# Differential scores from four 128-row matmuls, and a block's combination queued behind the next block's maxima

## The chip, the cores and the metric

One core of a Trainium2 chip runs the kernel; the other cores are idle. The metric is the device time of one execution in microseconds (us), median of several runs. The core has five engines with queues of their own: TensorE (PE, with weight loads, PEld, that overlap its matmuls), VectorE (DVE), ScalarE (ACT), GpSimd (POOL) and SyncE (SP), which here issues DMAs. A tile framework makes the semaphores, and its scheduler orders each engine's instructions before the run by its own estimates, following the order of the program text where nothing speaks against it. `keep_in_program_order` pins one instruction behind the instruction that was written just before it for the same engine.

## The reference

A two-layer encoder on 1024 tokens of width 1024, in float32. Layer 0 is a pooling mixer beside latent attention, layer 1 differential attention; each layer ends with a SwiGLU block. Only layer 1's attention is touched:

```python
s = jnp.einsum('bqhmd,bkhmd->mbhqk', qblk, k).astype(jnp.float32) * scale + bias[None, None]
p = jax.nn.softmax(s, axis=-1)
a = (p[0] - lam * p[1]).astype(v.dtype)
return jnp.einsum('bhqk,bkhe->bqhe', a, v)
...
o = rmsnorm(o, subln_g) * (1.0 - lam_init)
```

There are 8 heads; each has two maps (m = 0, 1) of 64 features, a bias that falls with distance, and values of 128 features.

## The kernel before

Matrix products keep float32 accuracy by splitting: each operand becomes hi (its rounding to fp32r) plus lo (the rest), and a product is hi x hi + hi x lo + lo x hi, three fp32r matmuls (`mm3`, lines L162 to L164). ACT makes hi by a copy, DVE lo by a subtraction.

In the attention of layer 1 the outer loops run over 8 heads h and 2 halves hf of the queries, 16 groups in all, four blocks of 128 queries (qt) each. A group begins with the scores of its first block (`diff_scores`), then runs the values of the group before (`diff_values`: per 128 keys four transposes of the blocks' weights e, L506, a hi and a lo copy, L509 and L510, and an `mm3` with V), and in between and after it the scores of its other three blocks. `fill(n)` puts n units of projection work for the next head (`qkv_work`; a unit is one `mm3` of one k-tile, 24 units a group) between these steps. Work handed to `defer` (lo subtractions, mostly) is issued by later fills, one a unit.

Scores of one block: for each half of the keys, two PSUM banks (m = 0, 1) out of three that rotate (`ps_s`). L1263 multiplies QS[m] = [q hi; q lo] (64 rows each) with KS[m] = [k hi; k hi]: 128 rows. L1266 adds q hi x k lo, with KL on rows 64m to 64m+63: 64 rows. L1268 on DVE adds the bias, takes the maximum and frees the bank. After both halves DVE makes the negative maximum (L1276), ACT the exponentials (L1281) with their sums l. Then DVE forms c = -lam l0 / l1 (L1285, L1286), and e0 + c e1 is made: on POOL for the first three blocks of a group (L1290, L1291), on DVE for the fourth (L1288). The transposes of the next group read it.

The operands come from `k_split` (L1151 scales, L1155 hi, an SP DMA that copies the hi half to the other 64 partitions, L1157 lo) and `q_split` (L1161, L1166, L1167, which writes lo straight to the other 64 partitions). `sub_norm` normalises a group's output; L1314 is its reciprocal of l0s, L1339 (`rest`) a deferred lo of its result. L136 is POOL's lo of projection weights, L134 the load of their raw chunks on SP's queue; three raw tiles rotate.

Of the kernel before, what the change touches and what calls it, by code (L numbers as in the profile page):

```python
# [34 lines left out]
def f(ap):  # L35
    return ap.bitcast(F32)
# [7 lines left out]
def encoder_trunk(ctx: ExitStack, tc: tile.TileContext, A: dict):  # L44
# [22 lines left out]
    def half(hf):  # L67
        return slice(hf * HT, (hf + 1) * HT)
# [4 lines left out]
    def tmp(name):  # L73
        return tpool.tile([P, HT], F32, tag="tm", name=name, bufs=6)
# [1061 lines left out]
    def defer(work):  # L1136

        later.append(work)

    def settle():  # L1140
        while later:
            later.pop(0)()

    def k_split(h, hf, ps):
        if hf == 0:
            heads[h]["k"] = (
                [qk.tile([P, T], F32R, tag=f"KS{m}", name=f"KS{m}_{h}", bufs=2) for m in range(2)],
                qk.tile([P, T], F32R, tag="KL", name=f"KL{h}", bufs=2))
        KS, KL = heads[h]["k"]
        t = tmp(f"kt{h}_{hf}")  # L1150
        dve.tensor_tensor(t, ps, rb[:, half(hf)], ALU.mult)  # L1151
        for m in range(2):
            r = slice(64 * m, 64 * m + 64)
            o = slice(64 - 64 * m, 128 - 64 * m)
            act.copy(KS[m][r, half(hf)], t[r, :])  # L1155
            nc.sync.dma_start(f(KS[m][o, half(hf)]), f(KS[m][r, half(hf)]))
            defer(lambda r=r, m=m: dve.tensor_tensor(KL[r, half(hf)], t[r, :], f(KS[m][r, half(hf)]), ALU.subtract))  # L1157

    def q_split(h, hf, ps):
        t = tmp(f"qt{h}_{hf}")  # L1160
        dve.scalar_tensor_tensor(t, ps, float(2.0 ** (h - 2)), rb[:, half(hf)], ALU.mult, ALU.mult)  # L1161
        QS = [qk.tile([P, HT], F32R, tag=f"QS{m}", name=f"QS{m}_{h}_{hf}", bufs=3) for m in range(2)]
        for m in range(2):
            r = slice(64 * m, 64 * m + 64)
            o = slice(64 - 64 * m, 128 - 64 * m)
            act.copy(QS[m][r, :], t[r, :])  # L1166
            defer(lambda r=r, m=m, o=o: dve.tensor_tensor(QS[m][o, :], t[r, :], f(QS[m][r, :]), ALU.subtract))  # L1167
        heads[h].setdefault("q", []).append(QS)

    def v_scale(h, hf, ps):  # L1170
        t = tmp(f"vt{h}_{hf}")
# [72 lines left out]
    def fill(n):  # L1244
        for _ in range(n):
            if later:
                later.pop(0)()
            if next(work, 0) == 0:
                settle()
                return  # L1250

    def diff_scores(h, qt, l0s):
        KS, KL = heads[h]["k"]
        slope = float(2.0 ** -(h + 1))
        c = blk(qt % 4)
        k0 = 896 - P * qt
        e = [at.tile([P, T], F32, tag=f"e{m}", name=f"e{m}_{h}_{qt}", bufs=(6, 2)[m]) for m in range(2)]
        mx = [spool.tile([P, 2], F32, tag="mx", name=f"mx{m}_{h}_{qt}") for m in range(2)]
        QS = heads[h]["q"][qt // 4]
        for hf in range(2):  # L1260
            ps = [ps_s(f"s{m}_{h}_{qt}_{hf}") for m in range(2)]
            for m in range(2):
                pe.matmul(ps[m], QS[m][:, c], KS[m][:, half(hf)], start=True, stop=False)  # L1263
            for m in range(2):
                r = slice(64 * m, 64 * m + 64)
                pe.matmul(ps[m], QS[m][r, c], KL[r, half(hf)], start=False, stop=True)  # L1266
            for m in range(2):
                dve.tensor_tensor_reduce(  # L1268
                    out=e[m][:, half(hf)], in0=ps[m], in1=nd[:, k0 + hf * HT : k0 + hf * HT + HT], scale=1.0,
                    scalar=-3.0e38, op0=ALU.add, op1=ALU.max, accum_out=mx[m][:, hf : hf + 1])  # L1270
            if hf == 0:
                fill(1)
        out = []
        for m in range(2):
            nm = spool.tile([P, 1], F32, tag="nm", name=f"nm{m}_{h}_{qt}")
            dve.tensor_scalar(nm, mx[m][:, 0:1], mx[m][:, 1:2], -slope, ALU.max, ALU.mult)  # L1276
            if m == 0:
                l = l0s[:, qt % 4 : qt % 4 + 1]
            else:
                l = spool.tile([P, 1], F32, tag="l", name=f"l1_{h}_{qt}")  # L1280
            act.activation(e[m], e[m], AF.Exp, bias=nm, scale=slope, accum_out=l)  # L1281
            out.append((e[m], l))
        (e0, l0), (e1, l1) = out
        c1 = spool.tile([P, 1], F32, tag="c1", name=f"c1_{h}_{qt}")
        dve.reciprocal(c1, l1)  # L1285
        dve.scalar_tensor_tensor(c1, l0, nlam, c1, ALU.mult, ALU.mult)  # L1286
        if qt % 4 == 3:
            dve.scalar_tensor_tensor(e0, e1, c1, e0, ALU.mult, ALU.add)  # L1288
        else:
            pool.tensor_scalar(e1, e1, c1, 0.0, ALU.mult, ALU.add)  # L1290
            pool.tensor_tensor(e0, e0, e1, ALU.add)  # L1291
        return e0

    def diff_values(h, hf, es, l0s, between):
# [8 lines left out]
    def sub_norm(h, hf, o, l0s, last=False):  # L1303


        nat = ps_t(f"on{h}_{hf}")
        for j in range(4):
            pe.transpose(nat[:, blk(j)], o[:, blk(j)], ident)
        ss = spool.tile([P, 4], F32, tag="ss", name=f"ss{h}_{hf}", bufs=2)
        sq = tmp(f"osq{h}_{hf}")  # L1310
        for j in range(4):
            act.activation(sq[:, blk(j)], nat[:, blk(j)], AF.Square, accum_out=ss[:, j : j + 1])
        r0 = spool.tile([P, 4], F32, tag="r0", name=f"r0_{h}_{hf}", bufs=2)
        dve.reciprocal(r0, l0s)  # L1314
        v = spool.tile([P, 4], F32, tag="v", name=f"v_{h}_{hf}")
        dve.tensor_tensor(v, ss, r0, ALU.mult)
        dve.tensor_tensor(v, v, r0, ALU.mult)
        dve.tensor_scalar(v, v, 1.0 / P, EPS, ALU.mult, ALU.add)
        r = spool.tile([P, 4], F32, tag="r", name=f"r_{h}_{hf}")
        pool.tensor_tensor(r, v, mhalf, ALU.pow)  # L1320
        dve.tensor_tensor(r, r, r0, ALU.mult)
        y = tmp(f"yn{h}_{hf}")
        dve.tensor_tensor(
            y.rearrange("p (a b) -> p a b", a=4), nat.rearrange("p (a b) -> p a b", a=4),
            r.unsqueeze(2).broadcast_to([P, 4, P]), ALU.mult)
        yield
        yt = ps_t(f"yt{h}_{hf}")
        for j in range(4):
            pe.transpose(yt[:, blk(j)], y[:, blk(j)], ident)
        if h in y_t:  # L1330
            yh, yl = (t[:, half(hf)] for t in y_t[h])
        else:
            yh = at.tile([P, HT], F32R, tag="pth", name=f"yh{h}_{hf}", bufs=3)
            yl = at.tile([P, HT], F32R, tag="ptl", name=f"yl{h}_{hf}", bufs=3)
        act.activation(yh, yt, AF.Identity, scale=gsub)


        def rest():
            dve.scalar_tensor_tensor(yl, yt, gsub, f(yh), ALU.mult, ALU.subtract)  # L1339
            if h not in y_t:  # L1340
                nc.sync.dma_start(f(ysp[h, 1, :, half(hf)]), f(yl))

        if last:
            rest()
        else:
            defer(rest)
        if h not in y_t:
            nc.sync.dma_start(f(ysp[h, 0, :, half(hf)]), f(yh))
# [28 lines left out]
    for h in range(NH):  # L1377
        for hf in range(2):
            l0s = spool.tile([P, 4], F32, tag="l0s", name=f"l0s_{h}_{hf}")
            es = [diff_scores(h, 4 * hf, l0s)]  # L1380

            def between(kt):
                if h < NH - 1 or hf or kt > 3:
                    fill(1)
                if kt == 3:
                    es.append(diff_scores(h, 4 * hf + 1, l0s))

            if prev is None:
                fill(8)
                es.append(diff_scores(h, 1, l0s))  # L1390
                fill(4)
                es.append(diff_scores(h, 2, l0s))
                fill(4)
                es.append(diff_scores(h, 3, l0s))
                fill(8)
            else:
                if h < NH - 1 or hf:
                    fill(3)
                pv = diff_values(*prev, between)
                fill(1)  # L1400
                norm_o = sub_norm(*pv)
                next(norm_o)
                es.append(diff_scores(h, 4 * hf + 2, l0s))
                fill(2)
                es.append(diff_scores(h, 4 * hf + 3, l0s))
                if h == NH - 1 and hf == 1:
                    fill(1000)
                    ya.release()
                    yb = new_pool("yb", "right")
                    load_y(yb, range(4, 8))  # L1410
                fill(6)
                next(norm_o, None)
            prev = h, hf, es, l0s
        if h == NH - 2:
# [6 lines left out]
            for o in ftr:  # L1421
                nc.sync.dma_start(hT[o], hsp[o])
            work = out_work()
    norm_o = sub_norm(*diff_values(*prev, lambda kt: fill(2)), last=True)
    next(norm_o)
    fill(1000)
# [218 lines left out]
```

## Time and profile before

| what | us |
|---|---|
| median of 3 runs | 2613.55 (2607.86 to 2615.01) |
| profiled execution | 2614.45 |
| its span, first to last instruction | 2612.7 |
| layer 1's attention, from its first groups to the end of its last scores | 1215 to 1842 of the span |

The rows below are from that one execution. Times in a timeline are microseconds from the span's start; "busy" of PE runs to modelled ends of overlapping matmuls, so starts tell more than lengths. A bracket behind a row is the idle time of that engine before it and what ended it. "issue" as releaser means that the profile shows nothing that the engine waited for.

### The profile page before, as it was taken

How to read it: one execution, taken by the hardware profiler on the slowest of the kernel's cores; microseconds unless marked ns; L12 is line 12 of the kernel's file. 1: busy time of each engine (PE TensorE's matmuls, PEld its weight loads, DVE VectorE, ACT ScalarE, POOL GpSimd, SP SyncE). 2: the span in 40 equal slices, each digit the busy share in tenths (PEclk: the TensorE clock that was granted, in tenths of full speed). 3: DMA queues.
4: the chain of work that ended last, by engine and by line, in shares of the span. 5: the costliest groups of instructions: out<-in, count | busy, mean ns of one | idle time of the engine just before them, and what ended most of it. 6: DMA issues, size and time to landing. Idle time of an engine off the chain costs nothing. (4 is left out here: it accounts for less than half of the span.)

```text
span 2612.7 us, 31389 instructions
## 1 busy us (share of the span) xinstructions
PE 2517.5 (96%) x11334; PEld 1989.8 (76%) x11334; DVE 1688.7 (65%) x2882; ACT 1060.5 (41%) x1866; POOL 757.8 (29%) x582
## 2 busy tenths in 40 slices
PE   8999999899999999999999999999989999999997
PEld 6787887678888888886666666666778888887886
DVE  7567777776666664554776776776586666666544
ACT  4236667533333331244555445554453333332222
POOL 4224444232222200033434344343343222220002
PEclk9999999999999999999999999999999999999998
DMA  3110001622222152321111111114352222215321
GB/s 130 37 45 15 17 9 43 163 95 73 91 79 85 69 173 81 113 98 60 37 45 37 45 41 33 41 42 165 117 141 97 81 89 77 93 56 183 113 73 65
DMA packets 127148, 205.50 MB, mean 79 GB/s; under 512 B 11280, under 2 KB 54288, under 8 KB 126992
## 3 DMA queue, kind: packets, MB, share of 16 engines
q1 hardware_dynamic: 120656, 187.76, 21.6%
q0 software_dynamic: 6336, 15.73, 2.4%
q8 instruction: 89, 1.46, 0.2%
q14 instruction: 67, 0.55, 0.1%
HBM read 145.25 MB, written 46.66 MB: 73 GB/s over the span
## 5 line engine op out<-in xcount | busy, mean ns | idle before, releaser
L163 PE MATMUL d<-al,whi_d 128*128 128x512 f32 x576 | 224.8, 390 | 0.4 <-DVE al L932 0.3
L164 PE MATMUL d<-ah,wlo_d 128*128 128x512 f32 x576 | 224.2, 389 | 0.0
L162 PE MATMUL d<-ah,whi_d 128*128 128x512 f32 x576 | 224.2, 389 | 0.0
L970 DVE TENSOR_TENSOR hd<-hd,d 128x512 f32<-128x512 f32 x160 | 109.6, 686 | 169.1 <-PE d L164 168.6
L776 POOL TENSOR_TENSOR s<-s,raw_a 128x512 f32<-128x512 f32 x88 | 116.3, 1322 | 327.6 <-DVE wlo_s L796 223.3
L509 ACT CAST pth<-pt 128x512 fp32r<-128x512 f32 x256 | 145.5, 586 | 155.5 <-PE pt L506 152.9
L510 DVE TENSOR_TENSOR ptl<-pt,pth 128x512 fp32r<-128x512 f32 x256 | 169.9, 686 | 53.1 <-ACT pth L509 51.6
L1268 DVE CUSTOM_DVE_ANT_0 e<-s,nd 128x512 f32<-128x512 f32 x256 | 169.2, 686 | 42.3 <-PE s L1266 39.5
L776 POOL TENSOR_TENSOR s<-raw_a,raw_a 128x512 f32<-128x512 f32 x88 | 116.8, 1327 | 250.8 <-DVE wlo_s L796 194.4
L795 ACT CAST whi_s<-s 128x512 fp32r<-128x512 f32 x142 | 88.3, 622 | 235.0 <-PE p L163 218.2
L1281 ACT ACTIVATE e<-e,nm 128x1024 f32<-128x1024 f32 x128 | 146.4, 1147 | 69.5 <-DVE nm L1276 69.4
L506 PE MATMUL pt<-ident,e 128*128 128x128 f32 x1024 | 155.8, 280 | 9.2 <-POOL e L500 4.7
L506 PEld LDWEIGHTS pt<-ident,e 128*128 128x128 f32 x1024 | 124.6, 144 | 48.0 <-DVE ptl L510 11.2
L1290 POOL TENSOR_SCALAR e<-e,c 128x1024 f32<-128x1024 f32 x48 | 57.4, 1196 | 273.4 <-ACT pth L509 97.3
L163 PEld LDWEIGHTS d<-al,whi_d 128*128 128x128 f32 x576 | 108.1, 188 | 24.5 <-DVE al L932 2.2
L162 PEld LDWEIGHTS d<-ah,whi_d 128*128 128x128 f32 x576 | 108.1, 188 | 22.3
L164 PEld LDWEIGHTS d<-ah,wlo_d 128*128 128x128 f32 x576 | 108.1, 188 | 22.3
L954 ACT CAST whi_d<-raw_d 128x512 fp32r<-128x512 f32 x72 | 44.4, 621 | 195.4 <-PE d L163 187.3
L795 ACT CAST whi_a<-raw_a 128x512 fp32r<-128x512 f32 x106 | 65.5, 621 | 134.5 <-PE p L163 131.5
L1263 PE MATMUL s<-KS,QS 128*128 128x512 f32 x256 | 96.0, 423 | 24.1 <-DVE mx L1268 23.2
L1291 POOL TENSOR_TENSOR e<-e,e 128x1024 f32<-128x1024 f32 x48 | 116.9, 2435 | 3.4
L796 DVE TENSOR_TENSOR wlo_s<-s,whi_s 128x512 fp32r<-128x512 f32 x142 | 115.7, 816 | 1.5 <-ACT whi_s L795 1.4
(501 smaller groups left out, 6998.5 us busy)
## 6 DMA issues: line engine op xcount, KB each, us to landing
raw_a<-in_w_gate_dram SPq DMA_DIRECT2D x88, 256.0 KB, 2.8
raw_a<-in_w_up_dram SPq DMA_DIRECT2D x88, 256.0 KB, 2.6
asp<-u SPq DMA_DIRECT2D x40, 512.0 KB, 2.9
raw_d<-in_w_down_dram SPq DMA_DIRECT2D x80, 256.0 KB, 2.7
araw<-asp SPq DMA_DIRECT2D x40, 512.0 KB, 4.0
hd<-hs POOLq DMA_DIRECT2D x16, 512.0 KB, 8.3
acc_f<-sq_f POOLq DMA_DIRECT2D x28, 256.0 KB, 4.1
hT<-in_xT_dram SPq DMA_DIRECT2D x16, 256.0 KB, 5.4
```

The source lines that it names most:

```text
L162: pe.matmul(ps, sh, mh, start=start, stop=False, skip_group_check=onto)
L163: pe.matmul(ps, sh, ml, start=False, stop=False, skip_group_check=onto)
L164: pe.matmul(ps, sl, mh, start=False, stop=stop, skip_group_check=onto)
L506: pe.transpose(pt[:, blk(j)], es[j][:, blk(kt)], ident)
L509: act.copy(hi, pt)
L510: dve.tensor_tensor(lo, pt, f(hi), ALU.subtract)
L776: pool.tensor_tensor(t, r[ff, a], r[ff, b], op)
L795: pin(act.copy(hi, self.raws[ff, n]))
L796: pin(dve.tensor_tensor(lo, self.raws[ff, n], f(hi), ALU.subtract))
L1268: dve.tensor_tensor_reduce(out=e[m][:, half(hf)], in0=ps[m], in1=nd[:, k0 + hf * HT : k0 + hf * HT + HT], scale=1.0, scalar=-3.0e38, op0=A ...
L1281: act.activation(e[m], e[m], AF.Exp, bias=nm, scale=slope, accum_out=l)
L1291: pool.tensor_tensor(e0, e0, e1, ALU.add)
```

## The change

`k_split` builds X[m], 128 partitions: k hi on rows 64m and up, k lo on the other 64, which DVE writes there directly; the DMA that doubled k hi goes. `q_split` builds two operands a map, [hi; hi] and [lo; lo]; the second half of each is a DMA on SP's queue from the first. `diff_scores` multiplies both with X[m]: (hi + lo) x (hi + lo), four products in two 128-row matmuls a map and key half. For the second half's queries of every head but the first, the split (`q_operands`) is called only after the next head's first scores, with its casts and subtractions pinned. The fourth block's combination (`combine`) is put on a list, `tail`, and called by `end_tail` in the next group's first scores, behind the maxima of the first key half, or after the loops; its reciprocal and that of `sub_norm` are pinned.

```diff
--- before.py
+++ after.py
@@ -1141,31 +1141,54 @@
         while later:
             later.pop(0)()
+    def rows(m):
+        return slice(64 * m, 64 * m + 64), slice(64 - 64 * m, 128 - 64 * m)
     def k_split(h, hf, ps):
         if hf == 0:
-            heads[h]["k"] = (
-                [qk.tile([P, T], F32R, tag=f"KS{m}", name=f"KS{m}_{h}", bufs=2) for m in range(2)],
-                qk.tile([P, T], F32R, tag="KL", name=f"KL{h}", bufs=2))
-        KS, KL = heads[h]["k"]
+            heads[h]["k"] = [qk.tile([P, T], F32R, tag=f"X{m}", name=f"X{m}_{h}", bufs=2) for m in range(2)]
+        X = heads[h]["k"]
         t = tmp(f"kt{h}_{hf}")
         dve.tensor_tensor(t, ps, rb[:, half(hf)], ALU.mult)
         for m in range(2):
-            r = slice(64 * m, 64 * m + 64)
-            o = slice(64 - 64 * m, 128 - 64 * m)
-            act.copy(KS[m][r, half(hf)], t[r, :])
-            nc.sync.dma_start(f(KS[m][o, half(hf)]), f(KS[m][r, half(hf)]))
-            defer(lambda r=r, m=m: dve.tensor_tensor(KL[r, half(hf)], t[r, :], f(KS[m][r, half(hf)]), ALU.subtract))
+            r, o = rows(m)
+            act.copy(X[m][r, half(hf)], t[r, :])
+            defer(lambda r=r, o=o, m=m: dve.tensor_tensor(
+                X[m][o, half(hf)], t[r, :], f(X[m][r, half(hf)]), ALU.subtract))
     def q_split(h, hf, ps):
-        t = tmp(f"qt{h}_{hf}")
+        if hf and h:
+            t = qk.tile([P, HT], F32, tag="tq", name=f"qt{h}_{hf}")
+        else:
+            t = tmp(f"qt{h}_{hf}")
         dve.scalar_tensor_tensor(t, ps, float(2.0 ** (h - 2)), rb[:, half(hf)], ALU.mult, ALU.mult)
-        QS = [qk.tile([P, HT], F32R, tag=f"QS{m}", name=f"QS{m}_{h}_{hf}", bufs=3) for m in range(2)]
+        if hf and h:
+            heads[h]["late"] = lambda: q_operands(h, hf, t)
+        else:
+            q_operands(h, hf, t)
+    def q_operands(h, hf, t):
+        Q = [[qk.tile([P, HT], F32R, tag=f"Q{w}{m}", name=f"Q{w}{m}_{h}_{hf}", bufs=2) for w in "hl"]
+             for m in range(2)]
+        pin = tc.keep_in_program_order if h and hf else lambda x: x
+        def low(m):
+            r, o = rows(m)
+            qh, ql = Q[m]
+            pin(dve.tensor_tensor(ql[r, :], t[r, :], f(qh[r, :]), ALU.subtract))
+            nc.sync.dma_start(f(ql[o, :]), f(ql[r, :]))
         for m in range(2):
-            r = slice(64 * m, 64 * m + 64)
-            o = slice(64 - 64 * m, 128 - 64 * m)
-            act.copy(QS[m][r, :], t[r, :])
-            defer(lambda r=r, m=m, o=o: dve.tensor_tensor(QS[m][o, :], t[r, :], f(QS[m][r, :]), ALU.subtract))
-        heads[h].setdefault("q", []).append(QS)
+            r, o = rows(m)
+            qh, ql = Q[m]
+            pin(act.copy(qh[r, :], t[r, :]))
+            nc.sync.dma_start(f(qh[o, :]), f(qh[r, :]))
+            defer(lambda m=m: low(m))
+        heads[h].setdefault("q", []).append(Q)
     def v_scale(h, hf, ps):
         t = tmp(f"vt{h}_{hf}")
@@ -1249,26 +1272,32 @@
                 settle()
                 return
+    tail = []
+    def end_tail():
+        while tail:
+            tail.pop(0)()
     def diff_scores(h, qt, l0s):
-        KS, KL = heads[h]["k"]
+        X = heads[h]["k"]
         slope = float(2.0 ** -(h + 1))
         c = blk(qt % 4)
         k0 = 896 - P * qt
         e = [at.tile([P, T], F32, tag=f"e{m}", name=f"e{m}_{h}_{qt}", bufs=(6, 2)[m]) for m in range(2)]
         mx = [spool.tile([P, 2], F32, tag="mx", name=f"mx{m}_{h}_{qt}") for m in range(2)]
-        QS = heads[h]["q"][qt // 4]
+        Q = heads[h]["q"][qt // 4]
         for hf in range(2):
             ps = [ps_s(f"s{m}_{h}_{qt}_{hf}") for m in range(2)]
             for m in range(2):
-                pe.matmul(ps[m], QS[m][:, c], KS[m][:, half(hf)], start=True, stop=False)
-            for m in range(2):
-                r = slice(64 * m, 64 * m + 64)
-                pe.matmul(ps[m], QS[m][r, c], KL[r, half(hf)], start=False, stop=True)
+                for i in range(2):
+                    pe.matmul(ps[m], Q[m][i][:, c], X[m][:, half(hf)], start=(i == 0), stop=(i == 1))
             for m in range(2):
                 dve.tensor_tensor_reduce(
                     out=e[m][:, half(hf)], in0=ps[m], in1=nd[:, k0 + hf * HT : k0 + hf * HT + HT], scale=1.0,
                     scalar=-3.0e38, op0=ALU.add, op1=ALU.max, accum_out=mx[m][:, hf : hf + 1])
             if hf == 0:
+                end_tail()
                 fill(1)
         out = []
         for m in range(2):
@@ -1282,13 +1311,22 @@
             out.append((e[m], l))
         (e0, l0), (e1, l1) = out
         c1 = spool.tile([P, 1], F32, tag="c1", name=f"c1_{h}_{qt}")
-        dve.reciprocal(c1, l1)
-        dve.scalar_tensor_tensor(c1, l0, nlam, c1, ALU.mult, ALU.mult)
+        def combine():
+            first = dve.reciprocal(c1, l1)
+            if qt % 4 == 3:
+                tc.keep_in_program_order(first)
+            dve.scalar_tensor_tensor(c1, l0, nlam, c1, ALU.mult, ALU.mult)
+            if qt % 4 == 3:
+                dve.scalar_tensor_tensor(e0, e1, c1, e0, ALU.mult, ALU.add)
+            else:
+                pool.tensor_scalar(e1, e1, c1, 0.0, ALU.mult, ALU.add)
+                pool.tensor_tensor(e0, e0, e1, ALU.add)
         if qt % 4 == 3:
-            dve.scalar_tensor_tensor(e0, e1, c1, e0, ALU.mult, ALU.add)
+            tail.append(combine)
         else:
-            pool.tensor_scalar(e1, e1, c1, 0.0, ALU.mult, ALU.add)
-            pool.tensor_tensor(e0, e0, e1, ALU.add)
+            combine()
         return e0
     def diff_values(h, hf, es, l0s, between):
@@ -1311,7 +1349,7 @@
         for j in range(4):
             act.activation(sq[:, blk(j)], nat[:, blk(j)], AF.Square, accum_out=ss[:, j : j + 1])
         r0 = spool.tile([P, 4], F32, tag="r0", name=f"r0_{h}_{hf}", bufs=2)
-        dve.reciprocal(r0, l0s)
+        tc.keep_in_program_order(dve.reciprocal(r0, l0s))
         v = spool.tile([P, 4], F32, tag="v", name=f"v_{h}_{hf}")
         dve.tensor_tensor(v, ss, r0, ALU.mult)
         dve.tensor_tensor(v, v, r0, ALU.mult)
@@ -1378,6 +1416,8 @@
         for hf in range(2):
             l0s = spool.tile([P, 4], F32, tag="l0s", name=f"l0s_{h}_{hf}")
             es = [diff_scores(h, 4 * hf, l0s)]
+            if hf == 0 and h:
+                heads[h].pop("late")()
             def between(kt):
                 if h < NH - 1 or hf or kt > 3:
@@ -1421,6 +1461,7 @@
             for o in ftr:
                 nc.sync.dma_start(hT[o], hsp[o])
             work = out_work()
+    end_tail()
     norm_o = sub_norm(*diff_values(*prev, lambda kt: fill(2)), last=True)
     next(norm_o)
     fill(1000)
```

## Rows read from the trace of the kernel before

**Rows 1.** The page's part 1: busy time, share of the span, instructions.
```profile
PE 2517.5 (96%) x11334; PEld 1989.8 (76%) x11334; DVE 1688.7 (65%) x2882; ACT 1060.5 (41%) x1866; POOL 757.8 (29%) x582
```
**Rows 2.** Busy time in one stretch: from:to, length, engines, PEclk, DMA share, GB/s.
```profile
1215.00:1842.00 627.00, 597.85 (x2688) 421.19 (x2688) 446.94 (x1127) 322.25 (x646) 250.23 (x159) 0.98 0.16 52
```
**Rows 3.** Waits of PEld, 1205 to 1842: total us, times, longest us.
```profile
PEld s L1266 <- issue: 49.6, 152, 0.7
PEld s L1263 <- DVE mx L1268: 34.6, 35, 2.1
...
PEld pt L506 <- POOL e L1291: 0.8, 1, 0.8
```
**Rows 4.** Timeline of PE: start, length, engine, line, operation, tiles, shapes, count.
```profile
1467.33 0.63 PE L1263 MATMUL s<-KS,QS 128*128 128x512 f32 x2
1467.89 0.49 PE L1266 MATMUL s<-KL,QS 64*128 64x512 f32 x2
...
1468.65 0.40 PE L163 MATMUL k<-al,whi_k 128*128 128x512 f32 x1
1468.89 0.40 PE L164 MATMUL k<-ah,wlo_k 128*128 128x512 f32 x1
```
**Rows 5.** Timeline of PE across a seam between two groups.
```profile
1436.68 0.71 PE L1263 MATMUL s<-KS,QS 128*128 128x512 f32 x2
1437.32 0.50 PE L1266 MATMUL s<-KL,QS 64*128 64x512 f32 x2
...
1438.57 0.40 PE L1263 MATMUL s<-KS,QS 128*128 128x512 f32 x1
...
1439.65 0.40 PE L163 MATMUL v<-al,whi_v 128*128 128x512 f32 x1
...
1440.36 0.39 PE L163 MATMUL v<-al,whi_v 128*128 128x512 f32 x1
1442.29 0.60 PE L1263 MATMUL s<-KS,QS 128*128 128x512 f32 x1 [1.54 <-DVE mx L1268]
```
**Rows 6.** Busy time behind that seam's stall, columns as in rows 2.
```profile
1442.00:1446.00 4.00, 3.71 (x9) 2.44 (x10) 3.32 (x12) 0.00 (x0) 0.00 (x0) 0.57 0.17 66
```
**Rows 7.** Timeline of DVE at the same seam.
```profile
1436.68 2.06 DVE L1286 SCALAR_TENSOR_TENSOR c<-l0s,nlam,c 128x1 f32<-128x1 f32 x1
...
1440.10 1.40 DVE L1167 TENSOR_TENSOR QS<-qt,QS 64x512 fp32r<-64x512 f32 x2
1441.53 0.69 DVE L1268 CUSTOM_DVE_ANT_0 e<-s,nd 128x512 f32<-128x512 f32 x1
```
**Rows 8.** Single lines, whole span: duration ns min/median/max, first and last start.
```profile
L1285 DVE RECIPROCAL c<-l x64: 155/164/166, 1220.0 to 1842.6; 128x1 f32<-128x1 f32 x64
...
L1286 DVE SCALAR_TENSOR_TENSOR c<-l0s,nlam,c x64: 209/220/2070, 1220.7 to 1842.8; 128x1 f32<-128x1 f32 x64
...
L1288 DVE SCALAR_TENSOR_TENSOR e<-e,c,e x16: 1283/1285/2269, 1237.7 to 1843.6; 128x1024 f32<-128x1024 f32 x16
```
**Rows 9.** Timeline of POOL at two seams.
```profile
1436.34 2.39 POOL L1291 TENSOR_TENSOR e<-e,e 128x1024 f32<-128x1024 f32 x1
...
1479.08 1.54 POOL L136 TENSOR_TENSOR wlo_v<-raw_v,whi_v 128x512 fp32r<-128x512 f32 x1 [0.94 <-ACT whi_v L135]
```
**Rows 10.** Timeline of PEld: the first and the last of twelve such stalls.
```profile
1283.07 0.19 PEld L1263 LDWEIGHTS s<-KS,QS 128*128 128x128 f32 x1 [1.97 <-DVE mx L1268]
...
1725.04 0.19 PEld L1263 LDWEIGHTS s<-KS,QS 128*128 128x128 f32 x1 [2.07 <-DVE mx L1268]
```
**Rows 11.** Timeline of DVE at the seam between a head's halves.
```profile
1479.40 2.49 DVE L1157 TENSOR_TENSOR KL<-kt,KS 64x512 fp32r<-64x512 f32 x2
1481.92 0.69 DVE L1268 CUSTOM_DVE_ANT_0 e<-s,nd 128x512 f32<-128x512 f32 x1
```
**Rows 12.** DMA issues of 1205 to 1842: count, KB each, median us to landing.
```profile
KS<-KS SPq DMA_DIRECT2D x30, 128.0 KB, 2.2
```
**Rows 13.** Waits of SP's queue, 1205 to 1842: total us, times, longest us.
```profile
SPq L134 <- POOL wlo_k L136: 155.8, 14, 20.4
```

## Prediction

> **What bounds the kernel now.** I read the page first: one core, PE (TensorE) busy 96% of a span of 2612.7 us [rows 1]. The change touches only the differential attention, so the second view is the busy time of that stretch, 1215 to 1842 us [rows 2]: PE 597.85 of 627 us, DVE 446.94, ACT 322.25, POOL 250.23, granted clock 0.98. PE sets the pace there, but its ends are modelled, so I next ask what idles it: the waits of its weight loads [rows 3]. Two entries stand out. Before the 64-row matmuls (L1266) it idles 49.6 us in 152 places with "issue" as releaser: it waits for nobody. Before the 128-row score matmuls (L1263) it waits 34.6 us, 35 times, for the maxima on DVE (L1268), which free the PSUM banks. The change acts on both.
>
> The first entry, in order of time on PE [rows 4]: two KS matmuls from 1467.33, the KL pair at 1467.89, then one L162, L163 at 1468.65, L164 at 1468.89. Where 128-row matmuls follow each other, a slot (start to start) is 0.24 (1468.65 to 1468.89); I use 0.235. The KL pair runs side by side (one row, x2, 0.49 in all), but with idle time around it: from the first KS to L163 are 1.32, and without it three slots would be 0.705. A KL matmul alone costs as much: KS at 1438.57, one KL, one L162, L163 at 1439.65 [rows 5].
>
> The second entry, at the seam between two groups of four query blocks: the last matmul starts at 1440.36, the next KS at 1442.29 [rows 5], and over 1442 to 1446 the granted clock is 0.57 [rows 6]: after the stall PE is mostly at the 1.2 GHz level. DVE meanwhile [rows 7]: L1286, whose median is 0.22 [rows 8], takes 2.06 until POOL's L1291 (1436.34, 2.39 long [rows 9]) ends; then come L1288 (1.28 [rows 8]) and two L1167 (1.40), and only at 1441.53 the maxima, whose scores were done near 1437.8 (L1266 at 1437.32, 0.50 long [rows 5]). Such stalls of about 2 us come twelve times, the first at 1283.07, the last at 1725.04 [rows 10], 441.97 / 11 = 40.2 apart, once a group.
>
> **The change, part by part.** Everything is summed against the profiled execution: 2614.45 us, span 2612.7, 1.75 around it; the median of the runs, 2613.55, is 0.9 lower.
>
> (a) Scores. 256 KS and 256 KL matmuls become 512 of 128 rows; arithmetic on ACT and DVE keeps its counts. 256 KL in 152 places means 104 pairs and 48 singles, if no place has more than two. Pair: from the first KS to L163 1.32 (1467.33 to 1468.65); after, five slots, 1.175: saves 0.145. Single: 1438.57 to 1439.65 is 1.08; after, three slots, 0.705: saves 0.375. 104 x 0.145 + 48 x 0.375 = 33. Some of this lies before one of the 35 waits for DVE, where PE would only wait longer; if all 35 hide 0.25 each, 24 is left. I take 30. The fourth product (low by low) is new, and is in those slots.
>
> This row speaks against a rule. The Trainium skill, "TensorEngine Tiling (Array Packing)", Theoretical Speedup, gives up to 2x for a contraction of at most 64 rows; by it a pair costs one slot and undoing it adds time. The same page's Key Properties say that changing the tiling mode drains the engine. The trace has both: the shared slot, and idle time around it that is larger; so the sum goes by rows 4 and 5. By the first rule alone the term would be +24 instead of -30 (rival 2).
>
> (b) The seam. Reciprocal, c and L1288 of the fourth block move behind the next block's first two maxima on DVE; the reciprocal of l0s is pinned into place. Late queries (second half, every head but the first): two ACT casts, two DVE subtractions (1.40 a pair [rows 7]) and four SP copies move behind the next head's first scores. At a seam like that of 1442 DVE could then take the maxima at about 1437.9 and PE loses nothing: 1.93 between starts less a slot is 1.70 back. At every other seam K's two subtractions stay ahead of the maxima: there L1157 took 2.49 for two and the maxima began at 1481.92 [rows 11], under a POOL operation of 1.54 at 1479.08 [rows 9]. Without L1286 and L1288 they can begin when POOL's earlier operation is over, some 1.3 earlier, or meet the same one; I leave 0.5 of the stall. Six seams at 1.70 and six at 1.2: 17.4, take 17 (14 to 20).
>
> (c) The clock. A granted clock of 0.98 over 627 us [rows 2] is 12.5 us of full clock lost (by rounding 9 to 16). Near one stall it is 0.43 x 4 = 1.7 [rows 6], so seven drops or so. If the stalls go, the drops should go with them; I take 9 (5 to 12), since shorter stalls stay.
>
> (d) What is late next. The first transposes (L506) of the next eight need e of the fourth block, which now comes later. On PE, from the first KS of the seam (1436.7 [rows 5]): four score slots, three of one unit of projection, four scores, nine of three units, 20 x 0.235 = 4.7: transposes at 1441.4. On DVE: two maxima from 1437.9, 1.3; then 0.16 + 0.22 + 1.28 [rows 8]: 1440.9. So it just fits. If the second two maxima go ahead (1.3), or an all-SBUF operation meets a POOL one (L1286 up to 2.07, L1288 up to 2.27 [rows 8]), PE waits up to 2.2. Fifteen seams at 0 to 2.2: 0 to 33; I take 0.6 each, 9, nearer the lower end, since the combination waits only for the two maxima: its exponentials are done by 1436.68, when L1286 starts now [rows 7].
>
> (e) SP and POOL. Thirty K copies in this stretch (two a half of a head; 128 KB, 2.2 us to landing [rows 12]) go, four Q copies a half come: about 32 more. They stand in SP's queue among the weight loads, which wait for POOL up to 20.4 us [rows 13], and ahead of the spills of y. By the order of the work units the first half's queries are ready about half a group (20 us) before use, the late ones most of a group; a copy stuck behind the longest wait would be late by 20.4 + 2.2 - 20 = 2.6, in a few places. I take nothing (0 to 9). POOL's own work stays. At the start the first scores wait for a copy (2.2) behind the subtraction instead of for L1167: 2 (0 to 5), with projection work of head 0 to cover it. Late ACT casts: ACT is idle half of the stretch [rows 2], nothing.
>
> Sum: -30 - 17 - 9 + 9 + 2 = -45, and 2 more from the other 23 waits for the maxima: 34.6 less twelve of 2.0 leaves 10 [rows 3, 10], of which a DVE with fewer stops may give back anything (0 to 10). That is -47. 2614.45 - 47 is 2567.5; 0.9 lower, for a median, **2567**. Best of all terms: -33 - 20 - 12 + 0 - 10 = -75, 2539. Worst: -24 - 14 - 5 + 33 + 5 + 9 = +4, not all at once; half-way to it from the sum is 2592.
>
> **The rivals.**
> 1. The seam's stall only changes its name: the maxima still come late (behind K's subtractions or whatever the scheduler puts there) or the transposes take up what was won. Then (a) alone is left, with 2 lost at the start: -28, 2585. For it: DVE is busy 71% of the stretch and serves in order. Against: at 1437.9 nothing but the moved work stood between DVE and the maxima.
> 2. Drains are free on the path: PE's idle time at the switches is slack that other waits would take, and the pair's shared slot is what counts. Then 104 more slots x 0.235 = +24, less 17 + 9, plus 11: +9, 2623. The page named under (a) gives this by its speedup rule. Against: "issue" waits for nobody, and starts after the switch are late each time.
> 3. Slower: the combination falls further back on DVE, behind the next two maxima (2 x 0.69) and two late subtractions (1.40) [rows 7]. Then e is ready at 1437.9 + 1.3 + 2.8 + (1.66 to 4.5 [rows 8]) = 1443.7 to 1446.5, against transposes at 1441.4: PE waits 2.3 to 5.1, with a clock drop of 1.7 each time; fifteen times 4.0 to 6.8 is 60 to 102. The gains are 30 + 17 + 9 = 56, so it decides above 3.7 us a seam, and gives 2617 to 2659. For it: the scheduler orders what isn't pinned by its own estimates. Against: the pin puts the combination behind one pair of maxima only, and the transposes now wait for e just once, 0.8 us [rows 3].
> 4. All goes well: nothing given back at the transposes, and the other waits for maxima gone too: 2539 to 2552.
>
> **How the numbers follow.** Forecast 0.62 (2552 to 2580), rival 1 0.18 (2575 to 2600), rival 4 0.08, rival 2 0.05, rival 3 0.07. The range 2541 to 2598 holds the forecast, nearly all of rivals 1 and 4, and leaves 2 in 10 for the rest and for sizes I have wrong. About 0.3% (8 us) is what a measurement of this kernel can tell from no change: faster than 2605.7 takes forecast, rival 4 and nearly all of rival 1, 0.87; same 0.05; slower 0.08.
>
> **What would show it.** Right: no "issue" idle before score matmuls, 512 of them at 0.235; no wait near 2 us of PE for L1268 at the seams; a granted clock of 0.99 or more over the stretch; the fourth block's reciprocal behind two maxima on DVE; stretch about 47 shorter, nothing else changed. Wrong: transposes waiting for DVE's combination, scores waiting for Q copies, the seam's stall under K's subtractions, or score slots well over 0.235.

## The result and the profile after

| kernel | median of its runs, us | ratio to before, 95% interval |
|---|---|---|
| before, in the same runs | 2614.28 | |
| after | 2566.32 (2565.24 to 2566.88) | 0.982 [0.9803, 0.9836] |

Forecast 2567, from 2541 to 2598. The profiled execution took 2566.88, its span 2564.8 against 2612.7. The time went where the change is: the last score matmul began at 1838.1 before and at 1786.8 after, 51.3 earlier, with the same start of 1206.6 for the first.

The page's part 1, the answer to [rows 1]:

```profile
PE 2471.6 (96%) x11334; PEld 2004.5 (78%) x11334; DVE 1667.5 (65%) x2882; ACT 1060.4 (41%) x1866; POOL 761.0 (30%) x582
```

Counts of instructions are the same on every engine. Busy time by stretch, columns as in [rows 2]; the second is the stretch of [rows 2] cut to its new length.

```profile
1202.00:1250.00 48.00, 44.47 (x202) 34.42 (x203) 33.55 (x90) 27.22 (x46) 23.91 (x15) 1.00 0.22 63
1215.00:1785.00 570.00, 546.63 (x2641) 430.75 (x2640) 419.02 (x1101) 314.39 (x634) 251.98 (x157) 1.00 0.20 63
```

The granted clock, 0.98 in [rows 2], rounds to 1.00. DVE is now busy 419.02 of 570, 74%, against 71%.

The waits of PEld from 1205 to 1800 (total, times, longest), the answer to [rows 3]:

```profile
PEld s L1294 <- DVE mx L1296: 28.2, 37, 1.6
PEld o L162 <- ACT pth L509: 10.3, 27, 0.7
PEld pt L506 <- DVE ptl L510: 7.9, 13, 1.0
PEld pt L506 <- PE v L163: 6.1, 6, 1.0
...
PEld pt L506 <- DVE e L1321: 2.7, 9, 0.4
PEld s L1294 <- issue: 0.4, 1, 0.4
```

The 49.6 us of idle time that waited for nobody are down to 0.4. Before had 152 more such waits, 37.8 us in ten smaller entries, 145 of them right behind a 64-row matmul or pair; they are gone as well. The largest of them (PEld, 1205 to 1842):

```profile
PEld k L162 <- issue: 9.5, 39, 0.2
```

The waits for maxima are down by 6.4 only, and some of the others are new. But a weight load can wait while the matmul before it still runs: the 10.3 for ACT's pth are 0.3 in the list of PE's own waits. In that list the waits for maxima fall from 23.2 to 14.9, and all that have a releaser from 29.4 to 23.7 (before, 1205 to 1842; after, 1205 to 1800):

```profile
PE s L1263 <- DVE mx L1268: 23.2, 20, 1.7
PE s L1294 <- DVE mx L1296: 14.9, 24, 1.2
```

All 512 score matmuls have 128 rows, and their slots (PE's timeline) are 0.23 each, with nothing before or behind them:

```profile
1420.91 0.39 PE L1294 MATMUL s<-X,Qh 128*128 128x512 f32 x1
1421.14 0.40 PE L1294 MATMUL s<-X,Ql 128*128 128x512 f32 x1
1421.37 0.39 PE L1294 MATMUL s<-X,Qh 128*128 128x512 f32 x1
1421.60 0.39 PE L1294 MATMUL s<-X,Ql 128*128 128x512 f32 x1
1421.83 0.39 PE L162 MATMUL v<-ah,whi_v 128*128 128x512 f32 x1
```

DVE at a seam between two heads, the answer to [rows 7]: two maxima come first, then the combination, which is a reciprocal, c (0.21; in [rows 7] it took 2.06) and L1321. A third maximum, at 1422.55, still goes ahead of L1321.

```profile
1419.95 0.69 DVE L1296 CUSTOM_DVE_ANT_0 e<-s,nd 128x512 f32<-128x512 f32 x1 [2.95 <-PE s L1294]
...
1421.70 0.16 DVE L1316 RECIPROCAL c<-l 128x1 f32<-128x1 f32 x1
...
1422.42 0.21 DVE L1319 SCALAR_TENSOR_TENSOR c<-l0s,nlam,c 128x1 f32<-128x1 f32 x1
1422.55 0.68 DVE L1296 CUSTOM_DVE_ANT_0 e<-s,nd 128x512 f32<-128x512 f32 x1
1423.16 1.28 DVE L1321 SCALAR_TENSOR_TENSOR e<-e,c,e 128x1024 f32<-128x1024 f32 x1
```

DVE here waits for PE's scores (2.95), where in [rows 5] PE waited for DVE. At a seam between a head's halves, K's subtractions still stand ahead of the maxima (1.97, shorter than the 2.49 of [rows 11]; DVE's timeline):

```profile
1381.43 1.97 DVE L1158 TENSOR_TENSOR X<-kt,X 64x512 fp32r<-64x512 f32 x2 [2.22 <-ACT X L1157]
1383.43 0.69 DVE L1296 CUSTOM_DVE_ANT_0 e<-s,nd 128x512 f32<-128x512 f32 x1
```

PE still waits there, 0.89, and 0.83 to 0.90 at six such seams (PEld's timeline):

```profile
1384.18 0.19 PEld L1294 LDWEIGHTS s<-X,Qh 128*128 128x128 f32 x1 [0.89 <-DVE mx L1296]
```

Two waits are new and come once a head. In the fourth block of a head's second half, L1359, a 128x4 product, takes 1.25 beside a POOL operation (in before, as L1321, it never took more than 0.17), then L1361 follows, and only then the maxima, for which the weight load waits 1.56 (PE itself 1.14). First DVE's timeline, then POOL's, then PEld's:

```profile
1411.40 1.25 DVE L1359 TENSOR_TENSOR r<-r,r 128x4 f32<-128x4 f32 x1 [0.53 <-POOL r L1358]
1412.69 0.68 DVE L1361 TENSOR_TENSOR yn<-on,r 128x512 f32<-128x512 f32 x1
1413.41 0.68 DVE L1296 CUSTOM_DVE_ANT_0 e<-s,nd 128x512 f32<-128x512 f32 x1
```
```profile
1411.34 1.29 POOL L136 TENSOR_TENSOR wlo_k<-raw_k,whi_k 128x512 fp32r<-128x512 f32 x1
```
```profile
1414.15 0.19 PEld L1294 LDWEIGHTS s<-X,Qh 128*128 128x128 f32 x1 [1.56 <-DVE mx L1296]
```

And behind a seam between heads the late low parts of the queries (2.22 for two) hold up L510, the split of the transposed probabilities, and the next transposes wait for it (DVE's timeline, then PEld's). The releaser named is PE's own L163, which had ended; the order in time speaks for DVE, and two runs below have no such wait: the one without late queries, and the one with these low parts on POOL.

```profile
1428.32 2.22 DVE L1182 TENSOR_TENSOR Ql<-qt,Qh 64x512 fp32r<-64x512 f32 x2
1430.56 1.29 DVE L510 TENSOR_TENSOR ptl<-pt,pth 128x512 fp32r<-128x512 f32 x2
```
```profile
1431.37 0.20 PEld L506 LDWEIGHTS pt<-ident,e 128*128 128x128 f32 x2 [1.02 <-PE v L163]
```

### The profile page after: what moved, and what is told of

Read it like the earlier page. It is cut to its first block, busy times and chain, and to the rows that moved or that the text cites. A ratio compares the mean times of both kernels' runs of the same rounds, so it can differ in the third digit from the quotient of the medians.

```text
span 2564.8 us, 31514 instructions
## 1 busy us (share of the span) xinstructions
PE 2471.6 (96%) x11334; PEld 2004.5 (78%) x11334; DVE 1667.5 (65%) x2882; ACT 1060.4 (41%) x1866; POOL 761.0 (30%) x582
## 5 line engine op out<-in xcount | busy, mean ns | idle before, releaser
L163 PE MATMUL d<-al,whi_d 128*128 128x512 f32 x576 | 224.7, 390 | 1.2 <-DVE al L932 1.2
L510 DVE TENSOR_TENSOR ptl<-pt,pth 128x512 fp32r<-128x512 f32 x256 | 169.8, 686 | 36.3 <-ACT pth L509 34.9
L163 PEld LDWEIGHTS d<-al,whi_d 128*128 128x128 f32 x576 | 108.1, 188 | 25.1 <-DVE al L932 3.1
L1294 PE MATMUL s<-X,Qh 128*128 128x512 f32 x256 | 105.6, 414 | 16.1 <-DVE mx L1296 14.9
```

What stands on the lines that cost most here:

```text
L163: pe.matmul(ps, sh, ml, start=False, stop=False, skip_group_check=onto)
L510: dve.tensor_tensor(lo, pt, f(hi), ALU.subtract)
```

## The experiments

Each kernel was timed in five rounds beside the kernel before. A distance in us below is that of the ratios, times 2612.

My theory: the drains around the 64-row matmuls give some 30, the moved combination with the clock some 17 net of the transposes' waits. Against it: the seam's stall changes its name only (all of it is the scores), or the shared slot is what counts (the scores cost time).

**The scores alone** (after, without the tail and both pins):

```diff
-                end_tail()
...
-            if qt % 4 == 3:
-                tc.keep_in_program_order(first)
...
-        if qt % 4 == 3:
-            tail.append(combine)
-        else:
-            combine()
+        combine()
...
-        tc.keep_in_program_order(dve.reciprocal(r0, l0s))
+        dve.reciprocal(r0, l0s)
...
-    end_tail()
```

> The four 128-row matmuls and the late queries, without the moved combination and without the pins of the two reciprocals. Theory (switching the array between 64 and 128 rows costs idle time, the seam's stall and the clock's drops come from the combination): 28 to 35 us below the kernel before, 2580 to 2586; the 'issue' idle before the score matmuls goes from 49.6 us to under 2; about twelve stalls near 2 us at the seams and a granted clock of 0.98 stay. Rival (the idle time at the switches is slack, only the pair's shared slot counts): 0 to 24 us above the kernel before.

Measured: 2586.47, 0.9902 [0.9887, 0.9917], 26 below before, a little less than the 28 of the theory.

**The tail alone** (before, with `tail`, `end_tail` and both pins of after):

```diff
             if hf == 0:
+                end_tail()
                 fill(1)
...
+        if qt % 4 == 3:
+            tail.append(combine)
+        else:
+            combine()
...
```

> The kernel before with only the moved combination and the two pins; scores as before (128 rows and 64 rows). Theory: seams win up to 20, the clock 9 to 12, but half of the seams keep a stall under K's subtractions and other waits of PE for DVE grow: 15 to 25 us below the kernel before; granted clock 0.99 or more over 1215 to 1842; 'issue' before L1266 still near 50 us. Rival (the seam is what the whole gain of 48 comes from): 40 us or more below.

Measured: 2594.79, 0.9935 [0.9923, 0.9947], 17 below before. The two sum to 43 where both together gave 47: nearly additive, so both halves of the theory hold in size. "Only the scores" falls. The late queries were not in this one, and at its seam between heads the queries' two subtractions take 2.98 ahead of the maxima (DVE's timeline):

```profile
1429.88 2.98 DVE L1167 TENSOR_TENSOR QS<-qt,QS 64x512 fp32r<-64x512 f32 x2 [2.46 <-ACT QS L1166]
```

**128 rows alone** (before, one line; it adds the other map's low-by-low product to the score, which is small):

```diff
-                r = slice(64 * m, 64 * m + 64)
-                pe.matmul(ps[m], QS[m][r, c], KL[r, half(hf)], start=False, stop=True)
+                pe.matmul(ps[m], QS[m][:, c], KL[:, half(hf)], start=False, stop=True)
```

> The kernel before with one thing changed: the second score matmul takes all 128 rows of QS and KL (it adds the small term q lo x k lo of the other map, so the scores are not quite the same sum). Copies, subtractions, queues and order of work stay as in before; only the array's tiling in 256 matmuls changes. Theory: 104 x 0.145 + 48 x 0.375 = 33, less what lies before waits: 24 to 37 us below the kernel before. Rival (drains are free, the shared slot is lost): +24, 2638.

Measured: 2583.98, 0.9897 [0.9882, 0.9911], 27 below before. No operand or copy changed, only the rows; and from the first score to the last, the 2690 matmuls and DVE's 1125 operations come in the order of before. This is the cleanest of the runs. Waits of PEld in the same stretch as [rows 3]:

```profile
PEld s L1263 <- DVE mx L1267: 51.3, 38, 2.7
...
PEld s L1263 <- issue: 0.6, 1, 0.6
```

"issue" goes from 49.6 to 0.6, and the waits for maxima grow from 34.6 to 51.3 (in PE's own list from 23.2 to 35.1): PE's slots gave back some 39 to 44, of which 12 to 17 came back as waits for a DVE that was no faster. The gain is also that of the scores alone (26): the new operands and their copies neither gain nor cost anything that can be told.

**Back to 64 rows** (after, with the second product on 64 rows, low by low left out):

```diff
-                for i in range(2):
-                    pe.matmul(ps[m], Q[m][i][:, c], X[m][:, half(hf)], start=(i == 0), stop=(i == 1))
+                pe.matmul(ps[m], Q[m][0][:, c], X[m][:, half(hf)], start=True, stop=False)
+            for m in range(2):
+                r, o = rows(m)
+                pe.matmul(ps[m], Q[m][1][r, c], X[m][r, half(hf)], start=False, stop=True)
```

> The changed kernel with its second score matmul on 64 rows again (q lo x k hi; low by low is left out), both maps next to each other in the text. DVE, ACT, SP and the seam as in the changed kernel. Theory: 15 to 37 us above the changed kernel, 2581 to 2603, with 'issue' idle before these matmuls back. Rival: about 24 us below it, 2542.

Measured: 2581.67, 0.9884 [0.9871, 0.9898], 17 above after. Waits of PEld:

```profile
PEld s L1296 <- issue: 47.4, 148, 0.4
PEld s L1293 <- DVE mx L1298: 15.1, 23, 1.1
```

The drains are back in full (47.4), and the waits for maxima fall by 13 (28.2 to 15.1): the same exchange, read the other way. But the scheduler also put PE's and DVE's instructions in another order here, against what I had expected, so it isn't shown how much of the 17 is the rows. The shared slot loses in both pairs, so rival 2 falls.

**Late queries undone** (after, split where it was):

```diff
...
-        if hf and h:
-            heads[h]["late"] = lambda: q_operands(h, hf, t)
-        else:
-            q_operands(h, hf, t)
+        q_operands(h, hf, t)
...
-        pin = tc.keep_in_program_order if h and hf else lambda x: x
+        pin = lambda x: x
...
-            if hf == 0 and h:
-                heads[h].pop("late")()
```

> The changed kernel with every query split at once (no late call, no pins on its casts and subtractions); two buffers a query operand as in the changed kernel. Theory: the late call is what keeps the seam between two heads free: without it two subtractions (1.4 to 2.1) stand ahead of the maxima again at six seams, and the 1.0 that the transposes wait behind the late subtractions (six times in the changed kernel) goes: 2 to 8 us above the changed kernel, 2568 to 2574. Rival: the late call costs more than it gives, 4 to 6 us below, 2560 to 2562.

Measured: 2566.52, 0.9823 [0.981, 0.9837]: as after, so neither my 2 to 8 above nor the rival's 4 to 6 below. The seam's stall is there again, and the transposes' wait of 1.02 is gone. This part of the change only moves a stall of the same price. PEld at the seam:

```profile
1422.62 0.19 PEld L1288 LDWEIGHTS s<-X,Qh 128*128 128x128 f32 x1 [1.78 <-DVE mx L1290]
```

**The two left-over waits, each relieved** (after): the small product on POOL; the low parts of the first half's keys behind the maxima; then both.

```diff
-        dve.tensor_tensor(r, r, r0, ALU.mult)
+        pool.tensor_tensor(r, r, r0, ALU.mult)
```

> The changed kernel with the product r x r0 of sub_norm (L1359) on POOL, which has just made r, instead of on DVE. Theory: the 1.56 us that PE waits for maxima once a head (1414.15 in the changed kernel) comes from DVE's L1359, which waits for POOL's r and then runs 1.25 beside POOL's L136; with it on POOL DVE goes straight on: 4 to 9 us below the changed kernel, 2557 to 2562, with that wait under 0.8. Rival: DVE's yn, which needs r, only waits longer for POOL: no change or up to 5 above.

Measured: 2568.64, 0.9832 [0.9818, 0.9845].

(`low` is the subtraction; `tail` is made earlier.)

```diff
...
+            if h and hf == 0:
+                tail.append(lambda low=low: tc.keep_in_program_order(low()))
+            else:
+                defer(low)
```

> The changed kernel with K's subtractions of the first half put on the tail list, behind the moved combination, and pinned there. Theory: the stall of 0.85 to 0.9 at the seam between a head's halves (seven times) is K's two subtractions ahead of the maxima; it goes: 3 to 6 us below the changed kernel, 2560 to 2563. Rival: the subtractions then delay the copies of the transposes' loop as the late queries do, 1.0 a seam: no change or up to 4 above.

Measured: 2570.45, 0.983 [0.9817, 0.9844].

> The changed kernel with both edits, r x r0 on POOL and K's first subtractions behind the combination. Theory: the two sum, 7 to 15 us below the changed kernel, 2551 to 2559. Rival: DVE only shifts its late work, within 3 us of the better of the two.

Measured: 2563.24, 0.981 [0.9795, 0.9824]. All three miss their forecasts (4 to 9, 3 to 6 and 7 to 15 below after): each alone gains nothing (3 above after by the ratios, inside the intervals), and both together are 3 below it, which can't be told from no change. With the product on POOL the fourth block's wait falls from 1.56 to 0.66 and that of the half seam grows to 1.98 (PEld, product on POOL); with the keys late, the half seam's wait is gone and the transposes wait 1.15 instead (the second list, PEld, keys late).

```profile
1414.07 0.19 PEld L1294 LDWEIGHTS s<-X,Qh 128*128 128x128 f32 x1 [0.66 <-DVE mx L1296]
1459.81 0.19 PEld L1294 LDWEIGHTS s<-X,Qh 128*128 128x128 f32 x1 [1.98 <-DVE mx L1296]
```
```profile
1467.52 0.20 PEld L506 LDWEIGHTS pt<-ident,e 128*128 128x128 f32 x2 [1.15 <-DVE ptl L510]
```

So a wait that I saw was not the price of its cause: with the one gone, another came up or grew by as much.

**The combination one pair of maxima later** (after), which tests term (d) and rival 3:

```diff
             if hf == 0:
-                end_tail()
                 fill(1)
+            else:
+                end_tail()
```

> The changed kernel with the moved combination called behind the maxima of the second key half instead of the first, pinned there: the slower rival's place, and the price of a late e. e then comes 1.4 to 2.2 later on DVE, and the transposes, which wait 0.2 to 0.4 for it in the changed kernel, would wait about 1.6 to 2.6 at fifteen seams. Theory (PE waits for e and nothing hides it): 15 to 40 us above the changed kernel, 2581 to 2606, with L506 waiting for DVE's e 20 us or more in all. Rival (PE has other matmuls, or DVE's later work gains what e loses): within 8 us of the changed kernel.

Measured: 2565.52, 0.9823 [0.981, 0.9837], as after: the theory's 15 to 40 falls, its rival holds. e comes later, but the scheduler put four projection matmuls between the sixth and the last two transposes, and the wait for e grows only from 2.7 to 5.4 (PE's timeline, then the wait's entry of 1205 to 1795):

```profile
1382.60 0.81 PE L506 MATMUL pt<-ident,e 128*128 128x128 f32 x6
1383.17 0.48 PE L162 MATMUL q<-ah,whi_q 128*128 128x512 f32 x1
...
1384.18 0.38 PE L506 MATMUL pt<-ident,e 128*128 128x128 f32 x2
```
```profile
PEld pt L506 <- DVE e L1322: 5.4, 13, 0.7
```

**Without the pin on the combination** (after):

```diff
-            if qt % 4 == 3:
-                tc.keep_in_program_order(first)
```

> The changed kernel without the pin on the fourth block's reciprocal (text order unchanged, the scheduler may issue it earlier). Theory: the scheduler takes the reciprocal and c as soon as it thinks them ready, ahead of the maxima, so that DVE stops for the exponentials and for POOL's L1291 there again: 5 to 20 us above the changed kernel. Rival: the place in the text alone does it: within 3 us.

Measured: 2584.15, 0.9893 [0.988, 0.9907], 19 above after, which is what the tail gave. The scheduler puts the combination ahead of the maxima again, and DVE even idles 2.01 for ACT in it; the waits for maxima are 51.8. The other pin, on `sub_norm`'s reciprocal, stayed; no run tests it alone. DVE's timeline:

```profile
1425.61 0.16 DVE L1316 RECIPROCAL c<-l 128x1 f32<-128x1 f32 x1 [2.01 <-ACT e L1310]
1425.81 1.86 DVE L1317 SCALAR_TENSOR_TENSOR c<-l0s,nlam,c 128x1 f32<-128x1 f32 x1
1427.70 1.28 DVE L1319 SCALAR_TENSOR_TENSOR e<-e,c,e 128x1024 f32<-128x1024 f32 x1
1428.90 0.68 DVE L1296 CUSTOM_DVE_ANT_0 e<-s,nd 128x512 f32<-128x512 f32 x1
```

**Less work on DVE** (after): the queries' low parts on POOL, alone and with the two edits above.

```diff
-            pin(dve.tensor_tensor(ql[r, :], t[r, :], f(qh[r, :]), ALU.subtract))
+            pin((pool if h else dve).tensor_tensor(ql[r, :], t[r, :], f(qh[r, :]), ALU.subtract))
```

> The changed kernel with the low subtractions of the queries of all heads but the first on POOL instead of DVE. Theory (DVE's two late subtractions, 2.2 beside a POOL operation, make the transposes' loop wait 1.0 once a head): that wait goes, 3 to 8 us below the changed kernel, 2558 to 2563. Rival (DVE and POOL hold each other up, and POOL's combinations come later): no change or up to 10 above.

Measured: 2563.04, 0.9815 [0.9801, 0.9828]: 1 below after, no difference that can be told (forecast: 3 to 8). DVE is busy only 399.40 of the 570 us from 1215 to 1785 (419.02 in after), and the waits for maxima are 28.7 (28.2): less load on DVE does not by itself shorten them.

> The changed kernel with r x r0 on POOL, K's first subtractions behind the combination, and the query lows on POOL. Theory: DVE is relieved in the three places where PE waited for it, 5 to 15 us below the changed kernel, 2551 to 2561. Rival: the waits move on as with one edit alone, within 4 us of it.

Measured: 2557.14 (2550.85 to 2558.95), 0.9789 [0.9776, 0.9803]: 8 below after, and the fastest of all; its interval ends where that of after, [0.9803, 0.9836], begins. In the same 570 us DVE is busy 394.73 instead of 419.02, while PE gets through 2668 matmuls instead of 2641; the waits for maxima are 18.5 (28.2), those of the transposes for L510 grow to 14.7 (7.9). DVE's load is about that of the query lows alone, so the gain takes the two reliefs as well. A window as [rows 2], then waits of PEld:

```profile
1215.00:1785.00 570.00, 553.03 (x2668) 436.24 (x2667) 394.73 (x1064) 318.07 (x637) 287.61 (x202) 1.00 0.20 64
```
```profile
PEld s L1299 <- DVE mx L1301: 18.5, 31, 1.5
PEld pt L506 <- DVE ptl L510: 14.7, 21, 1.0
```

## Why the prediction was right, and where only its sum was

The sum, -47, was met (-48 between the medians), and so were its halves as the runs give them: 26 to 30 for the scores (forecast 30), 17 to 21 for the rest (forecast 17). Inside these halves the terms miss in both directions and cancel, and that part is luck. The terms:

**(a) Scores, forecast -30: right in kind, gross a little too small.** The line edit alone gave 27, the part alone 26, and what after has over the tail alone is (0.9935 - 0.982) x 2612 = 30. What I had too small is the gross, because I took one row for each kind. Over the places of before at full granted clock and without another wait (PE's timeline; means, since they stand for a sum), a lone 64-row matmul costs 0.42 more than its slots (29 places; 0.37 to 0.40 in 19, near my 0.375, and 0.48 to 0.49 in ten), and a pair 0.185 (62 places, 0.13 to 0.25), not 0.145: 48 x 0.42 + 104 x 0.185 = 39, not 33. The line edit's 27 + 12 by PE's own list come to the same. And what DVE takes back is no fixed 0.25 a wait, 9 in all, but 12 to 17. Two errors that cancel. The Trainium skill, "TensorEngine Tiling (Array Packing)", Key Properties, says that switching the tiling mode drains the array; every run here agrees, with 47 to 50 us of "issue" idle ahead of score matmuls where 64-row ones stand among 128-row ones and under 1 where they don't.

**(b) The seam, forecast -17: right in place, its net size open.** Between heads the stall is gone, as foretold. Between a head's halves 0.9 is left, where I left 0.5. And waits that I expected to stay as they were did not: 1.56 in the fourth block, 1.02 behind the late queries. By the weight loads, all waits that have a releaser other than "issue" come to 55.5 us before and 60.7 after, summed over the views of [rows 3] and of after; by PE's own list they fall from 29.4 to 23.7. By my terms (b), (d), (e) and the 2 for other maxima they should have fallen by 8. The two lists do not agree even in sign, so this size is not shown.

**(c) The clock, forecast -9: too small.** I counted on shorter stalls keeping some of the drops; they kept none. In windows of 20 us from 1202 to 1842 the granted clock of before is 0.83 in the first and 0.91 in seven others, 16 us of full clock in all; after has 1.00 in every window up to 1802. With (a) at 39 and (c) at 16 that is 55, of which the stretch got 51.3: the waits would have grown by some 4, inside what the two lists under (b) leave open. Finer than that the trace doesn't part them.

**(d) Transposes, forecast +9: too dear in the fifteen groups I counted, 2.7 in nine places; but I left out the sixteenth.** After the last scores there is no next group to work behind: `end_tail` stands after the loops, the exponentials were over by 1791, and the combination ran at 1807.60, just when the transposes wanted it; in before it began 5.5 us after the last score, at 1843.60, and the transposes came at 1858.58. The transposes waited 2.63, and the granted clock over 1810 to 1814 was 0.72 (DVE's timeline, PEld's, a window):

```profile
1807.60 0.16 DVE L1316 RECIPROCAL c<-l 128x1 f32<-128x1 f32 x1
1807.79 0.95 DVE L1319 SCALAR_TENSOR_TENSOR c<-l0s,nlam,c 128x1 f32<-128x1 f32 x1
1808.78 1.28 DVE L1321 SCALAR_TENSOR_TENSOR e<-e,c,e 128x1024 f32<-128x1024 f32 x1
```
```profile
1810.11 0.14 PEld L506 LDWEIGHTS pt<-ident,e 128*128 128x128 f32 x1 [2.63 <-DVE e L1321]
```
```profile
1810.00:1814.00 4.00, 3.55 (x14) 2.63 (x15) 2.49 (x5) 1.76 (x3) 0.00 (x0) 0.72 1.01 407
```

That accounts for the 3.4 by which the span gained less (47.9) than the scores (51.3): 2.63, and 0.28 x 4 = 1.1 lost at the lower clock, as I read it. No run moved this call alone, so the two parts are argued. That the last round costs something the other runs bear out: from the last score's start to the end of the span take 771 to 775 us where the last combination comes early (before, the scores alone, the line edit, the run without the pin) and 775 to 780 in the ten where it comes late.

**(e) SP and the start, forecast +2: right in kind, but nothing of it shows.** The first score matmul waited for the copy of its queries (PE's timeline); in before PE had waited 0.9 for DVE there, and both began at 1206.6. No later score matmul waited for a copy.

```profile
1206.60 0.70 PE L1294 MATMUL s<-X,Qh 128*128 128x512 f32 x2 [1.21 <-DMA Qh<-Qh]
```

**The rivals.** "Only the name changes" is half true: it holds for the late queries (zero when undone) and for each single relief, and fails for the combination, worth 17 alone and 21 on top of the scores. Rival 2 failed wherever the rows changed: 27, 26 and 30 gained, 17 lost on the way back. Rival 3 had the wrong price: I held the transposes as fixed in PE's order, and when e came later still, other matmuls went between them. Its condition (the scheduler orders what isn't pinned) is real, but it works the other way: without the pin the combination goes ahead of the maxima, and the tail's gain is gone.

## What to carry to other kernels

An idle stretch whose releaser is "issue" around matmuls of another row count is the sign of a switch: compare slots from start to start with and without it before counting a shared slot as a gain. The sum of such waits is not its price: here 49.6 + 37.8 us of them stood for 39 us of slots. When one in-order engine is three quarters busy and feeds the bound one, moving one piece of its work may only move the wait, unless the moved step goes behind something that is wanted sooner and is pinned there. And a step that is put behind the next round's work needs a look at the last round, which has no next.

## What the runs showed of the hardware

A DVE operation on a few numbers can last as long as the POOL operation it meets: L1359, on 128x4, took 1.25 from 1411.40 while L136 ran for 1.29 from 1411.34, and both ended within 0.02. The Trainium skill, "SBUF — State Buffer", SBUF: two separate sides, says that a DVE operation with two SBUF inputs and a GpSimd one that reads SBUF shut each other out for whole instructions; this row agrees. In before it was c (2.06 in [rows 7]), and L1359 took 0.16 to 0.17 every time; in after c is out of that place, and the same loss came up under L1359, seven times of sixteen.

The lost clock went with the stalls and not with the drains. Over 1215 to 1785 the granted clock was 0.98 in before, still 0.98 with the line edit and 0.99 with the scores alone (drains gone, stalls left), 0.99 with the tail alone, and 1.00 in after. It was 1.00 too in the run back to 64 rows, where the 47.4 us of drains are back and no wait for maxima is longer than 1.1.
